# Squares of q in the up-projection: from ScalarE, in place in PSUM, to GpSimd, out of the copied q

## The chip, the cores and the metric

The kernel runs on one core of one Trainium2 chip. Five engines with queues of their own work in it: TensorE (PE, with PEld for the loading of its weights), VectorE (DVE), ScalarE (ACT), GpSimd (POOL) and SyncE (SP, which issues the DMAs). The metric is the device time of one execution in microseconds (us); less is better.

## The reference, cut to what matters

The program is one layer: a normalised input is projected, one half of the channels goes through a pooling branch, the other through latent attention, and both are gated, joined and projected back. The change lies in the latent attention, where q is made from its low-rank latent and then normalised for each head:

```
q = einsum('bsr,rd->bsd', rmsnorm(q_lat, g_q_lat), w_uq).reshape(B, S, N_HEADS, QK_HEAD)
kv = einsum('bsr,rd->bsd', rmsnorm(kv_lat, g_kv_lat), w_ukv).reshape(B, S, N_HEADS, QK_NOPE + V_HEAD)
...
q = rmsnorm(q, g_qnorm)      # over the 96 elements of a head
k = rmsnorm(k, g_knorm)
```

S is 1024 tokens, N_HEADS 8, QK_HEAD 96. So each token has 768 elements of q, and the norm needs, for each token and head, the sum of 96 squares.

## The kernel before, in words

Tokens lie on the 128 partitions in the up-projection: eight token tiles t = 0 to 7 of 128 tokens. For each tile, `up_tr(t)` turns the latent rows by three matmuls with the identity into the PSUM tile `pt` (one buffer in all), ScalarE copies it to `lth` (the part that the matmul's number format holds), and VectorE subtracts to get the rest, `ltl`. `up_tok(t)` then multiplies with the split weights: two PSUM tiles `pq` of four heads each (six matmuls each, 128 x 384), and two PSUM tiles `pk` (three matmuls each, 128 x 512), `pk0` for k and `pk1` for v. Three products stand for one: `lth` by the high weights, `lth` by the low ones, `ltl` by the high ones, so the third matmul of each group is the first that needs `ltl`.

What becomes of them, for each tile (lines of the program before):

- L550, ScalarE: `pq`, times the latent's scale `rq`, is copied to `QT[:, t]` in SBUF (twice, four heads each).
- L551, ScalarE: the square of `pq` times `rq` is written back over `pq` in PSUM (twice).
- L552, VectorE: the squares are summed over 96 elements into `ssq` (twice, 384 elements each).
- L559, VectorE: `KT[:, t]` from `pk0`; L561, ScalarE: the square of `pk0` in place; L562, VectorE: its sum into `ssq`.
- L563, ScalarE, and L564, VectorE: the two halves of `VT[:, t]` from `pk1`.

Then `up_norm` turns all of `ssq` into the factors `rqk` (L117 to L125, three Newton steps, then L573 and L574). Beside the token loop stands `gains_of_qk` (called at t = 1): small VectorE operations on a few columns, and on GpSimd eight products of 128 x 128 that make the rotation tables `TA`, `TB`, `krr`, `KB` (L512, L513). It uses 192 columns of `QT[:, 7]` as scratch before tile 7 is written. A second small chain on VectorE at the same place finishes the latents' norm (`rq`, `rlat`: L123 to L125) and the factor `rkv` (L487).

PSUM has seven banks here for `pq`, `pk` and the projections `fps` of the features, in a ring.

After the up-projection comes a stage that I call the feature stage: `fm_tile(i)` for i = 2 to 10 runs 48 matmuls of 128 x 512 for each of nine output tiles (L169), with weights that ScalarE (L146, `whi`) and VectorE (L147, `wlo`) split first; GpSimd folds the raw weights for the bias (`fm_fold`, L151 and L153). Interleaved with them is the pooling: `u` (L526, VectorE, from PSUM), running sums `s` on GpSimd (L608, L613), edges and difference on VectorE (L616, L617, L620), `dh` on ScalarE (L623), `dl` on VectorE (L624), the map `pps` on PE (L639) and its use `yp` (L640, VectorE). And on VectorE stands `up_tail(t)` for each token tile: `QT` and `KT` times `rqk` (L643, L644, L646) and the rotation (`ra`, `rbt`, L650 to L653). After it the attention runs.

The order of each engine's queue in the up-projection and the feature stage is not the order of the source: a scheduler sets it when the program is built, by its own estimates of what is ready when; from then on each engine takes its queue strictly in order. (The stage ahead and the attention stand under a schedule written by hand.)

Of the kernel before, what the change touches and what calls it, by code (L numbers as in the profile page):

```python
# [12 lines left out]
AF = mybir.ActivationFunctionType  # L13
ALU = mybir.AluOpType
AX = mybir.AxisListType
# [5 lines left out]
NK = 8  # L21
# [36 lines left out]
def body(ctx, tc, small, cond, xT, ada_sc, ada_sh, ada_gt, w_lat, w_fm, pool_w, w_uq, w_ukv, gains, pos, w_out, out):  # L58
    nc = tc.nc
    V, A, G, T, SY = nc.vector, nc.scalar, nc.gpsimd, nc.tensor, nc.sync  # L60
# [71 lines left out]
    def bk(name):  # L132
        return bank.tile([P, 512], F32, tag="b", name=name)
# [343 lines left out]
    QT = qp.tile([P, NK, H, HD], F32, tag="QT", name="QT")  # L477
    KT = qp.tile([P, NK, H, HD], F32, tag="KT", name="KT")
# [5 lines left out]
    ssq = upl.tile([P, 2, NK, H], F32, tag="ssq", name="ssq")  # L484
# [54 lines left out]
    def up_tok(t, lth, ltl):  # L539
        rq = rlat[:, 0, t:t + 1]  # L540
        rk = rlat[:, 1, t:t + 1]
        for n in range(2):
            pq = bk(f"pq{t}{n}")
            i = 0
            for j in range(2):
                for l, r in ((lth, wuqh), (lth, wuql), (ltl, wuqh)):
                    T.matmul(pq[:, :384], l[:, j, :], r[:, j, n * 384:(n + 1) * 384], start=(i == 0), stop=(i == 5))  # L547
                    i += 1
            pqv = pq[:, :384].rearrange("p (h d) -> p h d", h=4)
            A.activation(QT[:, t, n * 4:n * 4 + 4, :], pqv, AF.Copy, scale=rq)  # L550
            A.activation(pqv, pqv, AF.Square, scale=rq)  # L551
            V.tensor_reduce(ssq[:, 0, t, n * 4:n * 4 + 4], pqv, AX.X, ALU.add)  # L552
        pkv = []
        for n in range(2):
            pk = bk(f"pk{t}{n}")
            for i, (l, r) in enumerate(((lth, wkvh), (lth, wkvl), (ltl, wkvh))):
                T.matmul(pk, l[:, 2, :], r[:, n * 512:(n + 1) * 512], start=(i == 0), stop=(i == 2))  # L557
            pkv.append(pk.rearrange("p (h d) -> p h d", h=H))
        V.scalar_tensor_tensor(KT[:, t, :, 0:64], pkv[0], rk, ggk.unsqueeze(1).broadcast_to([P, H, 64]),  # L559
                               ALU.mult, ALU.mult)  # L560
        A.activation(pkv[0], pkv[0], AF.Square, scale=rk)  # L561
        V.tensor_reduce(ssq[:, 1, t, :], pkv[0], AX.X, ALU.add)  # L562
        A.activation(VT[:, t, :, 64:128], pkv[1], AF.Copy, scale=rkv[:, t:t + 1])  # L563
        V.scalar_tensor_tensor(VT[:, t, :, 0:64], pkv[1], rkv[:, t:t + 1], VT[:, t, :, 64:128],  # L564
                               ALU.mult, ALU.subtract)
        jk = upl.tile([P, 32], F32, tag="jk", name=f"jk{t}", bufs=2)
        A.activation(jk, lat[:, t, 384:416], AF.Square, accum_out=kr2[:, t:t + 1])
# [11 lines left out]
    for t in range(NK):  # L579
        if t == 1:  # L580
            gains_of_qk()
        if t == 2:
            fm_w[2] = fm_weights(2)
        nxt = up_tr(t + 1) if t + 1 < NK else None
        up_tok(t, *lt)
        lt = nxt
# [592 lines left out]
```

## Time and profile before

| | us |
|---|---|
| median of three runs | 494.69 (492.67 to 495.92) |
| the profiled execution, its own time | 494.58 |
| its span in the trace | 492.8 |
| what lies around the span | 1.8 |

| stretch of the trace (us from the start) | what runs |
|---|---|
| 84 to 117 | up-projection: tile 0 begins at 84.88 on PE, the last matmuls of tile 7 at 116.92 |
| 117 to 226 | feature stage, nine output tiles on PE |
| 226 to 493 | attention and output projection |

In the up-projection PE takes a token tile in 3.8 us. The page gives busy times of engines over the whole span; a stage is read from the rows of its own stretch of time. A row of the timeline has the start, the duration, the engine, the line, the operation, its output and inputs, and in brackets the idle time ahead of it with what ended it. Durations of neighbours on an engine overlap a little, so the distance from start to start is the better measure of what one costs.

### The profile page before, as it was taken

How to read it: one execution, taken by the hardware profiler on the slowest of the kernel's cores; microseconds unless marked ns; L12 is line 12 of the kernel's file. 1: busy time of each engine (PE TensorE's matmuls, PEld its weight loads, DVE VectorE, ACT ScalarE, POOL GpSimd, SP SyncE). 2: the span in 40 equal slices, each digit the busy share in tenths (PEclk: the TensorE clock that was granted, in tenths of full speed). 3: DMA queues.
4: the chain of work that ended last, by engine and by line, in shares of the span. 5: the costliest groups of instructions: out<-in, count | busy, mean ns of one | idle time of the engine just before them, and what ended most of it. 6: DMA issues, size and time to landing. Idle time of an engine off the chain costs nothing.

```text
span 492.8 us, 8658 instructions
## 1 busy us (share of the span) xinstructions
PE 466.9 (95%) x3468; PEld 357.2 (72%) x3468; DVE 353.4 (72%) x565; ACT 249.1 (51%) x322; POOL 222.9 (45%) x174
## 2 busy tenths in 40 slices
PE   5999998999999999999998999989999979999997
PEld 3999876898888888876565556556555658888886
DVE  4888858899999946475677887888867896813221
ACT  3756128895201111034788888788888961001000
POOL 1950031200161967736796797877959760000000
PEclk9999999899999999999999999999999999999999
DMA  8883541000102020127489879789993735743333
GB/s 294 331 323 145 171 147 53 35 2 5 50 1 92 0 91 1 43 59 156 111 136 192 171 147 182 141 168 167 208 214 57 172 140 228 273 170 129 128 129 128
DMA packets 117050, 66.40 MB, mean 135 GB/s; under 512 B 105873, under 2 KB 107793, under 8 KB 117010
## 3 DMA queue, kind: packets, MB, share of 16 engines
q1 hardware_dynamic: 117010, 65.85, 50.6%
q8 instruction: 27, 0.44, 0.4%
q14 instruction: 13, 0.11, 0.1%
HBM read 35.43 MB, written 4.19 MB: 80 GB/s over the span
## 4 chain that ended last, share of the span: by engine, by line
PE 52%; DVE 25%; ACT 7%; POOL 7%; issue 4%; DMA 4%; SPq 0%; DVEq 0%; ACTq 0%; POOLq 0%
PE ops L965 15%; PE fps L169 8%; PE st L798 6%; PE pq L547 3%; DVE bp L806 3%; POOL fraw L151 3%; ACT p L817 2%; PE rs L729 2%; DMA wlr<-in_w_lat 2%; PE pk L557 2%; PE st L802 2%; PE lps L233 2%; POOL s L613 2%; DVE ph L829 2%; ACT st L817 2%
## 5 line engine op out<-in xcount | busy, mean ns | idle before, releaser
L829 POOL TENSOR_TENSOR ph<-p,ph 128x1024 f16<-128x1024 f32 x49 | 106.2, 2176 | 12.1 <-ACT ph L822 11.7
L169 PE MATMUL fps<-xh,whi 128*128 128x512 f32 x192 | 62.0, 404 | 0.6 <-ACT whi L146 0.6
L169 PE MATMUL fps<-xh,wlo 128*128 128x512 f32 x192 | 59.3, 390 | 0.1
L169 PE MATMUL fps<-xl,whi 128*128 128x512 f32 x192 | 59.2, 390 | 0.0
L798 PE MATMUL st<-q,k 97*128 97x512 f16 x192 | 49.3, 379 | 7.3 <-ACT p L817 7.2
L822 ACT ACTIVATE ph<-p 128x1024 f16<-128x1024 f32 x49 | 51.6, 1052 | 0.5
L151 POOL TENSOR_TENSOR fraw<-fraw,shift 128x1024 f32<-128x1024 f32 x7 | 22.7, 3239 | 61.7 <-DVE wlo L147 54.8
L802 PE MATMUL st<-k,q 97*128 97x512 f16 x192 | 47.7, 379 | 1.8 <-DVE src L732 1.1
L806 DVE TENSOR_REDUCE bp<-st 128x1 f32<-128x1024 f32 x32 | 39.0, 1218 | 5.6 <-PE st L802 3.9
L169 PEld LDWEIGHTS fps<-xh,whi 128*128 128x128 f32 x192 | 35.5, 188 | 9.1 <-ACT whi L146 1.0
L169 PEld LDWEIGHTS fps<-xh,wlo 128*128 128x128 f32 x192 | 36.0, 188 | 8.0 <-DVE wlo L147 0.5
L169 PEld LDWEIGHTS fps<-xl,whi 128*128 128x128 f32 x192 | 36.1, 188 | 7.7
L817 ACT ACTIVATE p<-st,bp,esc 128x1024 f32<-128x1024 f32 x25 | 30.1, 1203 | 12.4 <-DVE bp L807 10.2
L926 ACT ACTIVATE owhi<-oraw 128x1024 fp32r<-128x1024 f32 (+1 forms) x10 | 8.8, 884 | 54.1 <-DMA oraw<-in_w_out 54.1
L798 PEld LDWEIGHTS <-k 97*128 97x128 f16 x192 | 16.6, 98 | 21.9 <-issue 8.6
L817 ACT ACTIVATE p<-st,ebias,esc 128x1024 f32<-128x1024 f32 x24 | 28.8, 1201 | 6.3 <-POOL ph L829 3.5
L623 ACT ACTIVATE dh<-s 128x1024 fp32r<-128x1024 f32 x4 | 4.3, 1064 | 52.0 <-DVE s L620 52.0
L802 PEld LDWEIGHTS <-q 97*128 97x128 f16 x192 | 16.7, 97 | 19.0 <-issue 3.9
L848 PE MATMUL av<-VT,pt 128*128 128x65 f16 x256 | 27.8, 193 | 1.3 <-DMA pt<-ph 1.3
L848 PEld LDWEIGHTS <-pt 128*128 128x128 f16 x256 | 23.7, 98 | 6.8 <-DMA pt<-ph 2.0
L850 PE MATMUL av<-VT,pt 128*128 128x65 f16 x256 | 27.7, 194 | 0.0
L849 PE MATMUL av<-VT,pt 128*128 128x64 f16 x256 | 27.6, 191 | 0.0
(299 smaller groups left out, 1227.7 us busy)
## 6 DMA issues: line engine op xcount, KB each, us to landing
fraw<-in_w_fm SPq DMA_DIRECT2D x12, 512.0 KB, 3.7
asc<-in_ada_sc SPq DMA_DIRECT2D x8, 512.0 KB, 6.2
xr<-in_xT SPq DMA_DIRECT2D x8, 512.0 KB, 5.2
ash<-in_ada_sh SPq DMA_DIRECT2D x8, 512.0 KB, 6.7
oraw<-in_w_out SPq DMA_DIRECT2D x8, 512.0 KB, 4.8
xres<-in_xT SPq DMA_DIRECT2D x8, 512.0 KB, 5.0
agt<-in_ada_gt SPq DMA_DIRECT2D x8, 512.0 KB, 5.8
out_dram<-xres SPq DMA_DIRECT2D x7, 512.0 KB, 3.0
```

What stands on the lines that cost most here:

```text
L151: G.tensor_tensor(pb, pb, shift.unsqueeze(2).broadcast_to([P, NK, P]), ALU.mult)
L169: T.matmul(ps[n], w[:, k, :], x_[k][:, n * 512:(n + 1) * 512], start=(k == order[0] and j == 0), stop=(k == order[-1] and j == 2))
L798: T.matmul(stt[i][:, n], l[:HW, kt * P:(kt + 1) * P], r[:HW, 0:512], start=(a == 0), stop=(a == 2))
L802: T.matmul(stt[i][:, n], l[:HW, qt * P:(qt + 1) * P], r[:HW, n * 512:(n + 1) * 512], start=(a == 0), stop=(a == 2))
L806: V.tensor_reduce(bps[i], stt[i], AX.XY, ALU.max)
L817: A.activation(pfs[i], st, AF.Exp, bias=bps.pop(i) if hf else ebias, scale=esc)
L822: A.activation(pas[i][:, 0], pfs[i], AF.Copy)
L829: (V if in_psum(i) else G).tensor_tensor(pas[i][:, 1], pfs[i], pas[i][:, 0], ALU.subtract)
L848: T.matmul(o_, hi, VT[:, kt, h, 64:129], start=kt == 0 and qt == 0, stop=False, skip_group_check=True)
L849: T.matmul(o_[:, 0:64], hi, VT[:, kt, h, 0:64], start=False, stop=False, skip_group_check=True)
L850: T.matmul(o_, lo, VT[:, kt, h, 64:129], start=False, stop=kt == NK - 1, skip_group_check=True)
L965: T.matmul(ps[d][n], w_[:, k, :], y_[k][:, n * 512:(n + 1) * 512], start=(k == 0 and j == 0), stop=(k == NK - 1 and j == 2))
```

## The change

For token tiles 0 to 6 the square in place (L551) and the two sums from PSUM (L552) go. In their place GpSimd multiplies the copied `QT[:, t]` by itself, all 768 elements in one instruction, and writes the squares to `KT[:, 7]`, which is free until tile 7 is made; VectorE then sums the 768 squares from there in one instruction. Tile 7 keeps the old way. One scratch serves seven tiles, so the square of a tile waits for the sum of the tile before it. The scale `rq` is in the copy already.

```
             A.activation(QT[:, t, n * 4:n * 4 + 4, :], pqv, AF.Copy, scale=rq)
-            A.activation(pqv, pqv, AF.Square, scale=rq)
-            V.tensor_reduce(ssq[:, 0, t, n * 4:n * 4 + 4], pqv, AX.X, ALU.add)
+            if t == NK - 1:
+                A.activation(pqv, pqv, AF.Square, scale=rq)
+                V.tensor_reduce(ssq[:, 0, t, n * 4:n * 4 + 4], pqv, AX.X, ALU.add)
+        if t < NK - 1:
+
+            G.tensor_tensor(KT[:, NK - 1], QT[:, t], QT[:, t], ALU.mult)
+            V.tensor_reduce(ssq[:, 0, t], KT[:, NK - 1], AX.X, ALU.add)
```

The scheduler answers with another order, and lines behind the edit stand five higher (L552 in `up_tok` becomes L557 for the new sum, L562 becomes L567, L640 becomes L645, and so on). Three places show it.

GpSimd's queue in the up-projection; `krr`, `KB`, `TA`, `TB` are the rotation tables. Before:

```order
L512 TENSOR_TENSOR krr<-krr,gn 128x8x16
L513 TENSOR_TENSOR KB<-KB,gn 128x8x16
L512 TENSOR_TENSOR TA<-krr,gn 128x8x16
L513 TENSOR_TENSOR TB<-KB,gn 128x8x16
L512 TENSOR_TENSOR TA<-krr,gn 128x8x16
L513 TENSOR_TENSOR TB<-KB,gn 128x8x16
L512 TENSOR_TENSOR krr<-krr,gn 128x8x16
L513 TENSOR_TENSOR KB<-KB,gn 128x8x16
```

And changed, where `KT<-QT` is the square:

```order
L512 TENSOR_TENSOR krr<-krr,gn 128x8x16
L513 TENSOR_TENSOR KB<-KB,gn 128x8x16
L556 TENSOR_TENSOR KT<-QT 128x768 x2
L512 TENSOR_TENSOR TA<-krr,gn 128x8x16
L513 TENSOR_TENSOR TB<-KB,gn 128x8x16
L512 TENSOR_TENSOR TA<-krr,gn 128x8x16
L513 TENSOR_TENSOR TB<-KB,gn 128x8x16
L512 TENSOR_TENSOR krr<-krr,gn 128x8x16
L513 TENSOR_TENSOR KB<-KB,gn 128x8x16
L556 TENSOR_TENSOR KT<-QT 128x768 x5
```

The squares of tiles 0 and 1 stand ahead of the six later table products, the other five behind them.

VectorE's queue at the start of the up-projection, up to `ltl` of tile 2, with what each instruction waits for (an engine's name stands for its semaphore). `pk_860` and `pk_858` are `pk0` of tile 0. Before:

```order
L562 TENSOR_REDUCE ssq<-pk_860 128x8 [waits Activation_49]
L125 SCALAR_TENSOR_TENSOR rlat<-rq_778,rlat 128x2x4 [waits DVE_49]
L501 TENSOR_SCALAR esc<-p_121 128x1
L502 TENSOR_SCALAR nesc<-p_121 128x1
L487 TENSOR_SCALAR rkv<-rlat,vsc 128x8 [waits DVE_49]
L503 RECIPROCAL ksc<-p_121 128x1
L507 TENSOR_SCALAR gn<-gn,p_121 128x32
L504 TENSOR_SCALAR ksc<-ksc 128x1 [waits DVE_49]
L536 TENSOR_TENSOR ltl_905<-pt_900,lth_904 128x384 [waits PE_49]
```

And changed:

```order
L501 TENSOR_SCALAR esc<-p_121 128x1 [waits DVE_49]
L557 TENSOR_REDUCE ssq<-KT 128x8 [waits Pool_49]
L123 TENSOR_TENSOR rq_778<-rlat 128x8 [waits DVE_49]
L567 TENSOR_REDUCE ssq<-pk_858 128x8 [waits Activation_49]
L124 SCALAR_TENSOR_TENSOR rq_778<-rq_778 128x8 [waits DVE_49]
L502 TENSOR_SCALAR nesc<-p_121 128x1
L503 RECIPROCAL ksc<-p_121 128x1
L125 SCALAR_TENSOR_TENSOR rlat<-rq_778,rlat 128x2x4 [waits DVE_49]
L507 TENSOR_SCALAR gn<-gn,p_121 128x32
L487 TENSOR_SCALAR rkv<-rlat,vsc 128x8 [waits DVE_49]
L504 TENSOR_SCALAR ksc<-ksc 128x1
L536 TENSOR_TENSOR ltl_903<-pt_898,lth_902 128x384 [waits PE_49]
```

The sum of tile 0's squares, which waits for GpSimd, now stands ahead of the last Newton steps, of the gains and of `ltl` of tile 2.

VectorE's queue in the feature stage, where the pooling's second group of channels is taken up. `u_1392` and `u_1378` are its `u`, `yp_801` the first group's result, `wlo_1429` and `wlo_1415` the weights of `fm_tile(5)`, `s_1` the second of its running sums. Before:

```order
L651 TENSOR_TENSOR rbt_1421<-QT,TB 128x256
L526 TENSOR_TENSOR u_1392<-fps_0_1326,rb 128x512
L526 TENSOR_TENSOR u_1392<-fps_1_1327,rb 128x512
L640 SCALAR_TENSOR_TENSOR yp_801<-pps_1382,small,yp_801 128x512
L640 SCALAR_TENSOR_TENSOR yp_801<-pps_1387,small,yp_801 128x512
L652 TENSOR_TENSOR QT<-ra_1420,rbt_1421 128x8x16
L653 TENSOR_TENSOR QT<-ra_1420,rbt_1421 128x8x16
L147 TENSOR_TENSOR wlo_1429<-fraw_1426,whi_1428 128x1024
L616 TENSOR_TENSOR s_1_1399<-s_1_1399,small 128x2
```

And changed:

```order
L656 TENSOR_TENSOR rbt_1407<-QT,TB 128x256
L648 TENSOR_TENSOR QT<-QT,rqk 128x768
L526 TENSOR_TENSOR u_1378<-fps_0_1312,rb 128x512
L645 SCALAR_TENSOR_TENSOR yp_801<-pps_1368,small,yp_801 128x512
L645 SCALAR_TENSOR_TENSOR yp_801<-pps_1373,small,yp_801 128x512
L526 TENSOR_TENSOR u_1378<-fps_1_1313,rb 128x512
L657 TENSOR_TENSOR QT<-ra_1406,rbt_1407 128x8x16
L658 TENSOR_TENSOR QT<-ra_1406,rbt_1407 128x8x16
L147 TENSOR_TENSOR wlo_1415<-fraw_1412,whi_1414 128x1024
L637 CAST pwh_1536<-pwr_1534 128x128
L649 TENSOR_TENSOR KT<-KT,rqk 128x8x64
L621 TENSOR_TENSOR s_1_1385<-s_1_1385,small 128x2
```

A `QT` product moved ahead of `u`, the second half of `u` moved behind the two `yp`, and `pwh` and a `KT` product moved ahead of the wait for `s_1`. Some 40 rows later, ahead of the third group's `u`, the instructions `rbt`, `QT`, `QT` (L651 to L653) of one token tile likewise moved from behind it to ahead of it.

## The prediction
> **What bounds the kernel now.** I read the page first, for the whole; then the busy times by stage; then PE's rows where it waits, and the chain of waits backward from there; last the timeline of the queues that the change touches.
>
> The page's span and busy times, and PE and VectorE in three stretches (busy us and instructions of each engine, granted clock, DMA):
>
> ```profile
> span 492.8 us, 8658 instructions
> PE 466.9 (95%) x3468; PEld 357.2 (72%) x3468; DVE 353.4 (72%) x565; ACT 249.1 (51%) x322; POOL 222.9 (45%) x174
> 89.00:117.00 28.00, 27.96 (x153) 25.19 (x152) 26.18 (x64) 25.88 (x52) 3.43 (x8) 1.00 0.00 1
> 117.00:211.00 94.00, 94.00 (x419) 77.46 (x418) 74.23 (x136) 16.59 (x19) 49.80 (x34) 1.00 0.11 37
> 211.00:227.00 16.00, 15.37 (x67) 11.67 (x67) 10.76 (x19) 5.26 (x7) 5.97 (x10) 1.00 0.45 98
> ```
>
> In the up-projection (first stretch) PE, ScalarE and VectorE are all over 92% busy, GpSimd 12%. In the feature stage PE is full for 94 us, and only behind it does it pause. That pause decides this case. PE's rows there, and the chain of waits that leads to them:
>
> ```profile
> 211.07 0.40 PE L639 MATMUL pps<-dh,pwl 128*128 128x512 f32 x1
> 212.04 0.74 PE L169 MATMUL fps<-xh,whi 128*128 128x512 f32 x2 [0.58 <-ACT whi L146]
> 213.31 0.50 PE L169 MATMUL fps<-xh,wlo 128*128 128x512 f32 x1
> ...
> 159.99 1.14 DVE wlo L147
> 161.20 10.00 POOL fraw L151
> 180.86 0.16 DVE s L616
> 187.35 1.91 POOL fraw L151
> 200.60 2.37 POOL s L613
> 202.99 1.23 DVE s L616
> 212.03 1.24 DVE wlo L147
> ```
>
> PE would go on at 211.3, waits for `whi`, and gets `wlo` at 213.31. Back from there the chain runs without a gap through `wlo`, GpSimd's sums, the fold at 161.20, and VectorE, whose timeline shows no idle time from 116 to 174. So although PE looks like the bound, the end of the feature stage is set by VectorE and GpSimd, with PE about 1.1 us late (211.3 plus the two matmul pairs that need no `wlo`, 0.9, would be 212.2). Whatever makes VectorE late at 117 comes out at 213; whatever makes it early gains at most that 1.1 us.
>
> **Removed.** ScalarE loses 14 squares, VectorE has seven long sums for 14 short ones:
>
> ```profile
> L551 ACT ACTIVATE pq<-pq,rlat x16: 547/560/582, 89.9 to 116.9; 128x384 f32<-128x384 f32 x16
> 105.45 0.69 DVE L562 TENSOR_REDUCE ssq<-pk 128x8 f32<-128x512 f32 x1 [0.40 <-ACT pk L561]
> 106.06 1.01 DVE L552 TENSOR_REDUCE ssq<-pq 128x4 f32<-128x384 f32 x2
> 106.99 0.74 DVE L559 SCALAR_TENSOR_TENSOR KT<-pk,rlat,ggk 128x512 f32<-128x512 f32 x1
> 107.65 0.74 DVE L564 SCALAR_TENSOR_TENSOR VT<-pk,rkv,VT 128x512 f16<-128x512 f32 x1
> 108.31 0.55 DVE L536 TENSOR_TENSOR ltl<-pt,lth 128x384 fp32r<-128x384 f32 x1
> ```
>
> 14 x 0.56 = 7.8 us leave ScalarE, but it is no longer than PE there, and no wait of PE in this stretch names it; I cost that at nothing (cover: PE's own 3.8 us per tile). On VectorE, start to start, a 384 sum takes 0.465, a 512 sum 0.61: 1.13 ns per element, so 768 take about 0.90, against 0.93 for the pair: equal. Per tile VectorE's work is 0.61 + 0.93 + 0.66 + 0.66 + 0.48 = 3.34 us before and 3.31 after, so half a us of a tile's 3.8 can absorb waits. The trace has no long sum from SBUF; were the new one free of the PSUM sums' fixed part, it would still cost 0.87, so I bound the gain at 0.5 us for all seven. The Trainium skill ("VectorE: DVE Perf Modes", the cycle table of the section on SBUF-source ops) gives 58 cycles plus the elements from SBUF and 120 plus the elements from PSUM: by that the pair costs 1.05 us, the long sum 0.86, and the stage would gain 1.3 us of VectorE time where I count 0.2. Here the 384 sum's 0.465 us is below its 0.525, so I keep the row.
>
> **Added: the square and its place in two queues.** The nearest row (the first) is an operation of the same size, the next the page's group of a larger one; then the rows of the startup and of the lock:
>
> ```profile
> 228.31 1.54 POOL L710 TENSOR_TENSOR src1h<-QT,src1h 128x768 f16<-128x768 f32 x1
> L829 POOL TENSOR_TENSOR ph<-p,ph 128x1024 f16<-128x1024 f32 x49 | 106.2, 2176 | 12.1 <-ACT ph L822 11.7
> 90.70 0.46 POOL L513 TENSOR_TENSOR KB<-KB,gn 128x128 f32<-128x128 f32 x1
> 93.79 0.55 DVE L536 TENSOR_TENSOR ltl<-pt,lth 128x384 fp32r<-128x384 f32 x1
> 94.39 0.55 PE L531 MATMUL pt<-ident,lat 128*128 128x128 f32 x3
> 122.47 2.06 POOL L608 TENSOR_TENSOR s<-u 128x1038 f32<-128x1038 f32 x1 [4.95 <-DVE rqk L112]
> 122.80 1.89 DVE L124 SCALAR_TENSOR_TENSOR rh<-rh 128x128 f32<-128x128 f32 x1
> ```
>
> The last two show the lock: a Newton step that takes 0.29 elsewhere took 1.89 because GpSimd was in an addition. VectorE operations with two SBUF inputs and GpSimd's exclude each other. (Those that read PSUM do not: the rows of `ltl` and the sums at 93.8 to 96 keep their length beside GpSimd's table products.)
>
> Startup, term A. GpSimd is free at 91.16, squares tile 0 until 92.7; the sum, ahead of everything else in VectorE's new order, ends at 93.6 (`QT`'s first copy starts at 89.4, both are done by 90.7). Then the square of tile 1 runs to 95.2 and holds the Newton step behind the k sum; the seven small instructions behind it take 0.6 as before, so `ltl` of tile 2 starts at 95.9 instead of 93.79. PE's `pt` of tile 3 waits for it (one buffer): 96.5 for 94.39. One matmul moved ahead of `pt` and a gap already there give back 0.4, so PE enters tile 2 about 1.7 late. Queued behind `ltl` are the `VT` halves, which hold PSUM banks; PE asks for those a tile later, so they add nothing.
>
> Steady tiles. With tile 4 of the trace:
>
> ```profile
> 102.49 0.42 PE L547 MATMUL pq<-wuqh,lth 128*128 128x384 f32 x1
> 106.06 0.49 PE L531 MATMUL pt<-ident,lat 128*128 128x128 f32 x3
> L550 ACT ACTIVATE QT<-pq,rlat x16: 574/583/592, 89.4 to 116.4; 128x384 f32<-128x384 f32 x16
> 119.96 0.33 DVE KB L520
> ```
>
> From the tile's start: the last `pq` ends at 2.25, its copy at 2.85, the square at 4.45 (1.54 and a handoff), then VectorE's sum 5.35, `VT` 6.0, k sum 6.6, `ltl` of two tiles on 7.1. PE asks for that `ltl`'s buffer at 3.81 + 3.57 = 7.4. So it holds, with 0.3 to spare; the wait of VectorE for GpSimd (0.5 to 0.7 a tile) is covered by its spare half us, nearly. I take one slip of 0.3. At the end `krr` (L519), now ahead of tile 6's sum, has two SBUF inputs and can stand behind the square of tile 6, which the next sum waits for anyway. VectorE reaches `KB` (119.96 before) 1.65 late if nothing more slips and 2.6 late if `krr` is held a full us. Term A: 2.2. Its bounds: 0.5 (no lock on the Newton step, waits all hidden), 3.
>
> **Moved in the feature stage.** Two places where VectorE and GpSimd overlapped:
>
> ```profile
> 144.07 1.28 DVE L526 TENSOR_TENSOR u<-fps,rb 128x512 f32<-128x512 f32 x2
> 145.49 1.92 POOL L608 TENSOR_TENSOR s<-u 128x1038 f32<-128x1038 f32 x1 [4.51 <-DVE u L526]
> 147.49 2.04 POOL L613 TENSOR_TENSOR s<-s 128x1036 f32<-128x1036 f32 x1
> 145.35 1.32 DVE yp L640 x2
> 142.54 0.60 DVE KT L644
> 152.23 0.87 DVE QT L643
> 150.54 0.15 DVE L616 TENSOR_TENSOR s<-s,small 128x2 f32<-128x2 f32 x1
> 169.35 1.27 DVE L526 TENSOR_TENSOR u<-fps,rb 128x512 f32<-128x512 f32 x2
> ```
>
> Term B. Before, GpSimd's two additions begin with `u` and run partly beside the two `yp`, which read PSUM. In the new order `u` is complete only after `QT` 0.87, `u` 0.60, `yp` 1.32, `u` 0.60: 144.07 + 3.4 = 147.46. From there all takes turns: GpSimd 1.92 + 1.93, VectorE `QT`, `QT` 0.4, `wlo` 1.13, `pwh` 0.14, `KT` 0.6: 6.1 us, to 153.6, for 150.54 before. Work that now lies ahead is 0.87 + 0.14 + 0.60 = 1.6, so the loss is 1.5. It does not depend on who goes first. Bounds: 0 (if GpSimd shares), 2.
>
> Term C. The fold at 161.20 stood behind VectorE's unbroken run of two-input products until `u` at 169.35 let it in. Three of them (0.34 + 0.20 + 0.20) now stand ahead of that `u`: 0.7. Bounds: -0.9 (that of the `QT` that left the run), 1.2. The Trainium skill ("SBUF — State Buffer", "Who interferes with whom") says that whoever starts first has the shared ports for one whole instruction. By that the fold waits for one product only, VectorE's `u` comes later instead, and C would be about 1.1; the row's 10.00 us, eight of them waiting, speaks for a longer hold.
>
> **Sum.** 2.2 + 1.5 + 0.7 = 4.4 us, all on the chain that ends at 213.31, where no slack is left; behind it PE is full to 226 and the attention follows in a fixed order, so it reaches the end. 494.58 + 4.4 = 499.0, against the profiled execution's own time, which is 0.1 below the median shown. That is 0.9%; I call a change measurable from 1% (4.9 us), so the likeliest verdict is no change, on the slow side.
>
> **Rivals.**
> - Slower by over 1%: the square is longer than I take. Place: the loop copy, square, sum, `ltl`. Slack 0.3, so it decides from about 1.9 us. At 2.2 (what the page's group `ph` takes for 128 x 1024) five tiles slip 0.3 each: 1.5 more, 500.5; at 3, 504. For it: the same addition took 2.06 at 122.47 and 1.92 at 145.49, so GpSimd is stretched by company. Against it: 1.54 for the same size. Chance 0.33 with the upper end of my own terms.
> - Hidden: the sums fill VectorE's idle half us, the Newton step slips between two squares, A falls to 0.5: 494.58 + 0.5 + 2.2 = 497.3; with B shared too, 495.5. For it: PE's stretch is full now. Chance 0.17.
> - Faster: ScalarE's 7.8 us free the banks sooner, VectorE ends early by its 0.5, and PE's pause at 211 shrinks: 494.0, at best 494.58 - 1.1 = 493.5, and more only if the order of the attention's work also fell better. Against it: PE is full from 89 to 211 already. Chance 0.05, of it 0.02 for over 1%.
>
> **Numbers.** My forecast holds 0.45, the rivals 0.33, 0.17 and 0.05. Time 499.0; range 495.4 (hidden, shared) to 502.5 (a square of about 2.6 us). That leaves out the faster case and a part of the hidden one below, and the long squares above, about 0.1 each. Faster by over 1% 0.02, within 0.45 + 0.17 + 0.03 = 0.65, slower 0.33.
>
> **What would show it.** A: `ltl` of tile 2 near 96 and PE's `pt` waiting for it; squares of 1.5 us; VectorE idle 0.5 ahead of each new sum. B: `wlo` of `fm_tile(5)` and its neighbours stretched, the s row at 153.6 + A. C: the third `u` 0.7 later again. PE's waits in the feature stage grow to near 4 us. Wrong if PE's `pt` never waits, if the VectorE chain ends the stage early, or if the attention's own length changes.

## The result, and the profile after

| | before | after |
|---|---|---|
| median, us (runs) | 494.57 (4 runs) | 499.55 (4 runs) |
| lowest to highest | 492.67 to 495.92 | 499.10 to 501.21 |
| the profiled execution, its span | 492.8 | 499.4 |

The ratio is 1.0118, with a 95% interval of 1.0091 to 1.0145: the change costs 1.2%. (In a second series, below, it was 1.0087, 1.0054 to 1.0120.) The page of the profile after, its span and the busy times:

```profile
span 499.4 us, 8644 instructions
PE 469.4 (94%) x3468; PEld 358.3 (72%) x3468; DVE 357.8 (72%) x558; ACT 243.9 (49%) x308; POOL 234.3 (47%) x181
```

The windows of the profile after, the three stretches of the prediction (busy us and instructions of PE, PEld, VectorE, ScalarE, GpSimd; granted clock, DMA share, GB/s):

```profile
89.00:117.00 28.00, 26.05 (x141) 23.15 (x141) 25.43 (x53) 18.84 (x34) 13.48 (x15) 1.00 0.00 1
117.00:211.00 94.00, 92.89 (x413) 76.15 (x412) 76.66 (x136) 16.58 (x20) 50.73 (x35) 1.00 0.11 37
211.00:227.00 16.00, 14.65 (x63) 11.22 (x62) 12.16 (x21) 5.26 (x5) 5.18 (x5) 1.00 0.16 46
```

ScalarE is 7.0 us lighter in the up-projection (25.88 to 18.84), GpSimd 10 us heavier (3.43 to 13.48), as meant. But PE, which had no gap there, now has 1.95 us of them. Where they come from is in the timeline of GpSimd, VectorE and PE, at the start and the end of the up-projection:

```profile
91.67 1.48 POOL L556 TENSOR_TENSOR KT<-QT 128x768 f32<-128x768 f32 x1
91.81 1.36 DVE L125 SCALAR_TENSOR_TENSOR rlat<-rq,rlat 128x8 f32<-128x8 f32 x1
93.18 0.95 DVE L557 TENSOR_REDUCE ssq<-KT 128x8 f32<-128x768 f32 x1
94.72 1.04 DVE L124 SCALAR_TENSOR_TENSOR rq<-rq 128x8 f32<-128x8 f32 x1
96.23 0.55 DVE L536 TENSOR_TENSOR ltl<-pt,lth 128x384 fp32r<-128x384 f32 x1
96.83 0.55 PE L531 MATMUL pt<-ident,lat 128*128 128x128 f32 x3 [1.53 <-DVE ltl L536]
...
101.49 0.95 DVE L557 TENSOR_REDUCE ssq<-KT 128x8 f32<-128x768 f32 x1 [0.81 <-POOL KT L556]
108.60 0.55 PE L531 MATMUL pt<-ident,lat 128*128 128x128 f32 x3 [0.25 <-DVE ltl L536]
116.03 1.46 DVE L519 TENSOR_TENSOR krr<-lat,krr 128x256 f32<-128x256 f32 x1
119.72 0.50 PE L562 MATMUL pk<-wkvh,lth 128*128 128x512 f32 x1 [0.50 <-DVE VT L569]
123.04 0.40 DVE L520 TENSOR_TENSOR KB<-lat,KB 128x256 f32<-128x256 f32 x1
```

The same places in the timeline of before (the second matmul of tile 2, then `krr` and `KB`), and the second matmul of tile 2 after:

```profile
95.13 0.34 PE L547 MATMUL pq<-wuql,lth 128*128 128x384 f32 x1
119.54 0.42 DVE L519 TENSOR_TENSOR krr<-lat,krr 128x256 f32<-128x256 f32 x1
119.87 0.42 DVE L520 TENSOR_TENSOR KB<-lat,KB 128x256 f32<-128x256 f32 x1
```

```profile
97.13 0.42 PE L547 MATMUL pq<-wuql,lth 128*128 128x384 f32 x1
```

Two Newton steps that take 0.16 undisturbed are held by squares (1.36 and 1.04), the sum stands ahead of `ltl`, and PE waits 1.53 for `ltl` of tile 2. Later VectorE waits 0.8 ahead of a sum, `krr` takes 1.46 for 0.42 beside the square of tile 6, and PE waits twice more (0.25 at 108.60, 0.50 at 119.72). The feature stage after, same view:

```profile
148.25 0.68 DVE L526 TENSOR_TENSOR u<-fps,rb 128x512 f32<-128x512 f32 x1
150.16 0.68 DVE L526 TENSOR_TENSOR u<-fps,rb 128x512 f32<-128x512 f32 x1
150.98 3.91 POOL L613 TENSOR_TENSOR s<-u 128x1038 f32<-128x1038 f32 x1 [6.69 <-DVE u L526]
154.97 1.92 POOL L618 TENSOR_TENSOR s<-s 128x1036 f32<-128x1036 f32 x1
156.92 0.16 DVE L621 TENSOR_TENSOR s<-s,small 128x2 f32<-128x2 f32 x1 [3.81 <-POOL s L618]
...
166.86 9.45 POOL L151 TENSOR_TENSOR fraw<-fraw,shift 128x1024 f32<-128x1024 f32 x1 [8.16 <-DVE wlo L147]
174.13 0.42 DVE L656 TENSOR_TENSOR rbt<-QT,TB 128x256 f32<-128x256 f32 x1
174.59 1.87 DVE L657 TENSOR_TENSOR QT<-ra,rbt 128x128 f32<-128x128 f32 x1
176.59 1.28 DVE L526 TENSOR_TENSOR u<-fps,rb 128x512 f32<-128x512 f32 x2
186.10 0.17 DVE L621 TENSOR_TENSOR s<-s,small 128x4 f32<-128x4 f32 x1 [1.87 <-POOL s L618]
...
217.21 0.73 PE L169 MATMUL fps<-xh,whi 128*128 128x512 f32 x2 [0.84 <-ACT whi L146]
```

The addition at 150.98 took 3.91 for 1.92, until VectorE had no product left, and VectorE then waited 3.81 for GpSimd. The fold at 166.86, which takes 1.9 alone, stood 7.6 us.

To compare traces that begin their work a little apart, I count from the first `pq` matmul of tile 0 (84.88 before, 85.22 after) to four marks: `KB` (L520), the first `s` row of the second and third pooling group (L616 before, L621 after), and the first `rs` matmul, with which the attention begins.

One thing has to be taken out first. In some executions PE's clock is halved right at the start of the up-projection. The same window of two traces, of the profile after and of a kernel below (`e2`) whose up-projection is that of before; the third number from the end is the granted clock:

```profile
86.00:88.00 2.00, 2.00 (x6) 1.60 (x6) 2.00 (x15) 1.69 (x8) 0.00 (x0) 0.50 0.77 258
```

```profile
86.00:88.00 2.00, 2.00 (x12) 1.57 (x11) 2.00 (x17) 1.79 (x5) 0.00 (x0) 1.00 0.61 229
```

The profiles before and after both have this dip, so they compare. Where the up-projection is otherwise unchanged, `KB` comes 34.99 after the first `pq` with the dip (before) and 33.56 without (`e2`): it costs 1.43, which I take off the marks of before for traces without a dip. (`e7`, whose up-projection is also that of before, has 33.52.) The dip does not fall on the same matmuls each time, and the changed kernel's `KB` is at 37.82 in one trace and 37.53 in the other, so marks of two traces compare to about 0.3. The Trainium skill ("TensorE: Matmul & The Clock Gate", "What's actually happening") says that the clock is either full or half, decided in free-running windows of about 3.4 us. The trace agrees: the mean clock from 85 to 89 is 0.57 after, which is 3.4 us at half.

A run's mean clock moves its time too. A straight line through the 194 fast runs of this study whose clock is on record (one run of `e2`, 502.18 us, was slow and is left out), with one offset for each kernel and one slope, gives 0.43 us per 0.001 of clock (runs lie between 0.986 and 1.000). Some kernels had their runs at lower clocks than others, so the table has each kernel's offset from the kernel before at equal clock, with its 95% interval, beside the plain ratio. The runs of the experiments come from three chips; the same line drawn for each chip alone moves no offset by more than 0.4.

| kernel | dip | `KB` | 2nd `s` | 3rd `s` | first `rs` | `rs` late by | time over before at equal clock | ratio, 95% interval |
|---|---|---|---|---|---|---|---|---|
| before | yes | 34.99 | 65.66 | 95.98 | 141.55 | | | |
| before, less 1.43 | no | 33.56 | 64.23 | 94.55 | 140.12 | | | |
| after | yes | 37.82 | 71.70 | 100.88 | 146.43 | 4.88 | 4.2 ± 0.4 (with e10) | 1.0118, 1.0091 to 1.0145 |
| e10 the same again | yes | 37.53 | 71.40 | 100.58 | 146.04 | 4.49 | | 1.0087, 1.0054 to 1.0120 |
| e1 order back | yes | 37.70 | 68.49 | 98.83 | 144.42 | 2.87 | 2.9 ± 0.6 | 1.0104, 1.0073 to 1.0134 |
| e2 order alone | no | 33.56 | 67.28 | 96.46 | 141.99 | 1.87 | 1.8 ± 0.4 | 1.0048, 1.0029 to 1.0066 |
| e3 sums behind | no | 34.61 | 65.43 | 95.75 | 142.31 | 2.19 | 1.7 ± 0.4 | 1.0043, 1.0025 to 1.0062 |
| e4 idle squares | no | 34.58 | 65.40 | 95.73 | 141.34 | 1.22 | 1.3 ± 0.4 | 1.0034, 1.0011 to 1.0056 |
| e5 tile 0 back | no | 33.91 | 64.71 | 95.03 | 141.59 | 1.47 | 1.3 ± 0.4 | 1.0039, 1.0016 to 1.0062 |
| e6 idle scalings | yes | 34.93 | 65.76 | 96.08 | 141.66 | 0.11 | 0.0 ± 0.4 | 0.9993, 0.9977 to 1.0009 |
| e7 `whi` first | no | 33.52 | 64.19 | 94.52 | 138.86 | -1.26 | -1.7 ± 0.4 | 0.9972, 0.9954 to 0.9990 |
| e8 both | no | 33.92 | 64.74 | 95.07 | 140.42 | 0.30 | 0.4 ± 0.4 | 1.0006, 0.9984 to 1.0028 |
| e9 free bank | yes | 36.63 | 67.46 | 97.78 | 142.11 | 0.56 | -1.3 ± 0.4 | 0.9981, 0.9956 to 1.0006 |

From these rows: the changed kernel is 2.83 late at `KB`, and 4.90 at the third `s`; then nothing is added (4.88 at `rs`). Of the 6.04 at the second `s`, 1.61 is work that now lies ahead of it, so 4.43 count there: 1.60 more than at `KB`, and 0.47 more come by the third. The profiled execution was the longest of its four and lost another 1.4 in the attention (267.75 from `rs` to the end, 266.37 before): its clock dipped a second time there, to a mean of 0.84 from 410 to 420. In e10, the same kernel, the two marks that matter come out alike: 2.54 late at `KB`, 1.59 more at the second `s`, 0.47 more at the third.

### The profile page after: what moved, and what is told of

It is laid out like the page before. It is cut to its first block, busy times and chain, and to the rows that moved or that the text cites. A ratio compares the mean times of both kernels' runs of the same rounds, so it can differ in the third digit from the quotient of the medians.

```text
span 499.4 us, 8644 instructions
## 1 busy us (share of the span) xinstructions
PE 469.4 (94%) x3468; PEld 358.3 (72%) x3468; DVE 357.8 (72%) x558; ACT 243.9 (49%) x308; POOL 234.3 (47%) x181
## 4 chain that ended last, share of the span: by engine, by line
PE 53%; DVE 25%; ACT 7%; POOL 6%; issue 4%; DMA 4%; SPq 0%; DVEq 0%; ACTq 0%; POOLq 0%
PE fps L169 15%; PE ops L970 15%; PE st L803 5%; PE st L807 3%; DVE bp L811 3%; DMA wlr<-in_w_lat 2%; ACT p L822 2%; PE rs L734 2%; PE lps L233 2%; POOL fraw L151 2%; DVE yq L914 1%; POOL ph L834 1%; DVE ph L834 1%; ACT st L822 1%; DMA pt<-ph 1%
## 5 line engine op out<-in xcount | busy, mean ns | idle before, releaser
L853 PE MATMUL av<-VT,ph 128*128 128x65 f16 x256 | 27.6, 193 | 0.0
```

Source lines behind the costliest of these rows:

```text
L853: T.matmul(o_, hi, VT[:, kt, h, 64:129], start=kt == 0 and qt == 0, stop=False, skip_group_check=True)
```

## The experiments

My theory was three separate losses: A in the up-projection, where VectorE's queue passes waits for GpSimd's squares on to PE; and B and C in the feature stage, where the same instructions stand in another order. The rivals were that the order alone costs the time (PE being full in the up-projection and absorbing its delay), that the up-projection alone costs it, and that GpSimd's company costs it wherever the sums stand.

The first two kernels hold VectorE's queue to a list. The numbers are those of its instructions counted from `krr` (L519); the added edges order the queue and make nothing wait:

```
+DVE_ORDER = (223, 195, 196, 186, 191, 224, 225, 231, 201, 202, 352, 203, 353, 382, 383, 207, 384, 387, 388,
...
+def keep_order(tc, nc, first):
+    n0 = int(first.name[2:])
+    dve = {int(i.name[2:]) - n0: i for i in nc.cur_bb.bb.instructions
+           if i.engine == first.engine and i.name[2:].isdigit()}
+    for p, q in zip(DVE_ORDER, DVE_ORDER[1:]):
+        tc.add_manual_dep(dve[q], dve[p].name,
+                          mybir.DependencyInfo(mybir.DependencyClass.NoSync, mybir.DependencyReason.DATA),
+                          reason="order")
```

### e1: the up-projection's part alone

The changed kernel with that list, the order of before from the second group's `u` to the third group's sums.

> The changed kernel, with VectorE's queue in the feature stage (from the second group's u to the third group's sums) held in the order of the kernel before: the up-projection's part of the change alone. My theory (three separate losses, A in the up-projection, B and C from the other order in the feature stage): KB is 2.8 us late against the kernel before, the s row of the second group is as late and no later, and the time is 494.6 + 2.8 = 497.4 (496.8 to 498.0). Rival 1, the feature stage's order alone costs time, since PE's full queue absorbs the up-projection: 494.6. Rival 2, the up-projection alone costs it and the order is harmless: 499.5.

Measured: 498.59 (6 runs) against 493.67 on the same chip, a ratio of 1.0104. Taken plainly, that is 4.9 and the second rival. But these six runs had a mean granted clock of 0.9925, those of before 0.998; at equal clock it is 2.9 ± 0.6, as the theory has it. The trace does not need that correction, since it is compared with a trace of the same dip: `KB` 2.71 late, the second `s` 2.83, the third 2.85, `rs` 2.87. What is late at `KB` comes out unchanged at the attention, and nothing is added. The first rival falls. This run does not tell which engine carries the delay: PE itself ends the up-projection 2.91 late (its last `pk` matmul, 34.95 after the first `pq` for 32.04).

### e2: the order alone

The kernel before with the changed kernel's list; not one instruction of the up-projection differs.

> The kernel before, without any change in the up-projection, with VectorE's queue in the feature stage held in the order of the changed kernel: terms B and C alone. My theory: KB where it was, the s row of the second group 1.6 us late beside the 1.6 of work that now lies ahead of it, the third group's s row about 2.1 late, time 494.6 + 2.1 = 496.7 (496.0 to 497.2). The order alone (rival 1): 499.5. Harmless order (rival 2): 494.6.

Measured: 1.8 ± 0.4 at equal clock, the plain ratio 1.0048. Its timeline, GpSimd and VectorE:

```profile
146.12 3.90 POOL L608 TENSOR_TENSOR s<-u 128x1038 f32<-128x1038 f32 x1 [6.69 <-DVE u L526]
152.05 0.16 DVE L616 TENSOR_TENSOR s<-s,small 128x2 f32<-128x2 f32 x1 [3.81 <-POOL s L613]
161.99 9.45 POOL L151 TENSOR_TENSOR fraw<-fraw,shift 128x1024 f32<-128x1024 f32 x1 [8.16 <-DVE wlo L147]
169.72 1.87 DVE L652 TENSOR_TENSOR QT<-ra,rbt 128x128 f32<-128x128 f32 x1
181.23 0.16 DVE L616 TENSOR_TENSOR s<-s,small 128x4 f32<-128x4 f32 x1 [1.87 <-POOL s L613]
```

These are the durations of the changed kernel (3.91, 3.81, 9.45, 1.87), without its up-projection. The second `s` is 3.05 late, less 1.61 of moved work 1.44: B. The third is 1.91 late: C is 0.47. PE ends this up-projection on time, so here it is the chain through VectorE and GpSimd that makes the attention late. The theory is confirmed and the second rival falls; 2.87 and 1.87 add up to 4.74, the change itself is 4.88 and 4.49 late in its two traces.

### e3: the sums behind `ltl`

The order of e1, and seven edges that put the sum of tile t behind `ltl` of tile t + 2, and `krr` behind the last k sum. The last edge undoes the move of `krr`.

```
+SUMS_BEHIND = ((-281, -329), (-234, -263), (-193, -216), (-152, -175), (-111, -134), (-70, -93), (-6, 0))
...
-    for p, q in zip(DVE_ORDER, DVE_ORDER[1:]):
+    for p, q in [*SUMS_BEHIND, *zip(DVE_ORDER, DVE_ORDER[1:])]:
```

> The changed kernel with the feature stage's order of before and with each of VectorE's new sums put behind the ltl of the tile after next, krr back behind the last k sum: GpSimd squares as much as in the change, but VectorE no longer stands waiting for it ahead of an ltl. My theory (VectorE's in-order queue passes the wait on): only the Newton step held by the first square is left, 1.1 us less PE's 0.4 of slack, so KB 0.7 late and 494.6 + 0.7 = 495.3 (494.6 to 496.0). Rival, GpSimd's squares slow the others wherever the sums stand: as with the first of these kernels, 497.4.

Measured: 1.7 ± 0.4, between the two. The trace divides it: `KB` is 1.05 late instead of 2.71, and stays so to the third `s` (1.20); from there to `rs` another 1.0 is lost. So the sums' place and `krr` account for 1.66 of A. A part of that comes by way of GpSimd's queue: the square of tile 1 waits for the sum of tile 0, so it now stands behind the six table products (93.96), where it holds no Newton step. What the other 1.0 ahead of the attention is, e5 and e9 show.

### e4: the squares' company alone

The kernel before, with squares that nobody reads:

```
+        if t < NK - 1:
+            G.tensor_tensor(KT[:, NK - 1], QT[:, t], QT[:, t], ALU.mult)
```

> The kernel before with seven squares of q on GpSimd that nobody reads, added to its own sums; every engine's queue is otherwise as before: the squares' company alone. My theory: a Newton step held by the first square, 1.1 us less PE's 0.4, no wait of VectorE for GpSimd after that: 495.3 (494.6 to 495.8). Rival, the squares' company is most of the up-projection's loss (VectorE's instructions or PE's matmuls get longer beside them): 2 us or more, 496.6 to 497.4.

Measured: 1.3 ± 0.4; `KB` 1.02 late, `rs` 1.22. The 1.02 is made at one place, in the timeline:

```profile
89.62 1.47 POOL L554 TENSOR_TENSOR KT<-QT 128x768 f32<-128x768 f32 x1
89.89 1.22 DVE L125 SCALAR_TENSOR_TENSOR rlat<-rq,rlat 128x8 f32<-128x8 f32 x1
91.73 0.48 PE L559 MATMUL pk<-wkvh,lth 128*128 128x512 f32 x1 [0.57 <-DVE rq L123]
```

One Newton step takes 1.22 for 0.16, and PE waits for what follows it already at the `pk` of tile 1. The 0.4 of slack that I had subtracted belongs to the changed kernel's PE queue, where a matmul moved ahead of `pt`; this kernel has the queue of before and is 1.01 late from that `pk` on. The other six squares hold nothing on the path (`KB` is no later than this one step). Squares cost by what they meet, not by being there.

### e5: tile 0 by ScalarE

e3, with the place of e4's loss taken away:

```
-            if t == NK - 1:
+            if t in (0, NK - 1):
...
-        if t < NK - 1:
+        if 0 < t < NK - 1:
```

> As the kernel with the sums behind ltl, and tile 0 squared by ScalarE and summed in two short sums as before the change, so that GpSimd squares tiles 1 to 6 only and nothing runs beside the startup's Newton steps. My theory (the 1.1 to 1.2 us that the two kernels with unhurried sums still lost are one Newton step held by the first square, 1.22 or 1.36 us for 0.16): ltl of tile 2 and KB where they were, and the time of the kernel before, within 0.4 at equal granted clock. Rival (each square costs a little): six sevenths of it are left, 1.0 over the kernel before.

Measured: 1.3 ± 0.4, which looks like the rival. The trace says otherwise: `ltl` of tile 2 is where it was (7.43 after the first `pq`, 7.44 in e2), `KB` is 0.35 late, the third `s` 0.48; what that 0.35 is, I did not find out (PE ends the up-projection on time, 30.63 after the first `pq` for 30.61 in e2). Then comes the same 1.0 as in e3, here in the timeline of VectorE and PE:

```profile
222.89 0.68 DVE L526 TENSOR_TENSOR gT<-fps,rb 128x512 f32<-128x512 f32 x1
223.62 0.50 PE L169 MATMUL fps<-xh,whi 128*128 128x512 f32 x1 [0.77 <-DVE gT L526]
```

By the programs' allocations the last feature tile (`fps11`) is written to PSUM banks 4 and 5. In the kernel before, tile 10, whose halves are evicted (`gT`) just ahead, lies in banks 3 and 1; in e3 and e5 it lies in 1 and 5. The ring of banks goes on from the up-projection, and there, by my reading, the sums' new place lets go of the banks in another order; e9 tests it. So PE waits for an eviction 100 us behind the edit.

### e6: a lock, but between which operations

e4 with one input in place of two:

```
-            G.tensor_tensor(KT[:, NK - 1], QT[:, t], QT[:, t], ALU.mult)
+            G.tensor_scalar(KT[:, NK - 1], QT[:, t], 2.0, None, ALU.mult)
```

> The kernel before with seven idle operations on GpSimd as in the kernel of the idle squares, but each reads one tensor (q times 2.0) in place of q times q; nobody reads them. If the lock is between VectorE's two-input products and any SBUF operation of GpSimd (rival): the Newton step beside the first is held as before, 1 us, and the time is 1.1 over the kernel before. If it takes an operation of two inputs on GpSimd's side too (my theory, from rows that show only such): the Newton step stays at 0.16 and the time is that of the kernel before within 0.4.

Measured: 0.0 ± 0.4, `rs` 0.11 late.

```profile
90.27 2.14 POOL L554 TENSOR_SCALAR KT<-QT 128x768 f32<-128x768 f32 x1
90.93 0.18 DVE L125 SCALAR_TENSOR_TENSOR rlat<-rq,rlat 128x8 f32<-128x8 f32 x1
91.72 0.14 DVE L124 SCALAR_TENSOR_TENSOR rq<-rq 128x8 f32<-128x8 f32 x1
```

The operation is longer (2.14 for 1.47), covers the same Newton steps, and holds none. The Trainium skill ("SBUF — State Buffer", "Who interferes with whom") says that a VectorE instruction with two SBUF inputs contends with a GpSimd instruction that reads SBUF; in these rows the GpSimd operation with one input does not hold it, and the rows decide. They are two small steps of one run.

### e7 and e8: the pause at 211

The kernel before, with the order of before and one edge on ScalarE (651 is the activation of `gT`, 656 is `whi` of the tenth weight tile); e8 has the same edge on e5.

```
+    act = {int(i.name[2:]) - n0: i for i in nc.cur_bb.bb.instructions
+           if i.engine == mybir.EngineType.Activation and i.name[2:].isdigit()}
+    tc.add_manual_dep(act[651], act[656].name,
+                      mybir.DependencyInfo(mybir.DependencyClass.NoSync, mybir.DependencyReason.DATA),
+                      reason="order")
```

> The kernel before with two instructions of ScalarE exchanged at the end of the feature stage: whi of the tenth weight tile ahead of the bias and activation of gT, so that PE's pause at 211 no longer waits for ScalarE's queue. My theory: whi starts near 209.8 for 210.95, wlo ends 1.1 earlier, the pause is gone, and the time is 1.1 below the kernel before (492.6 where that is 493.7). Rival: gT is wanted, or whi's buffer is free, no earlier, and the time is unchanged.

> The repaired change (tile 0 by ScalarE, the sums behind ltl, the feature stage's order of before) and the exchange on ScalarE together. My theory: the repaired change costs nothing and brings nothing, since PE is the bound in the up-projection, so the time is that of the exchange alone, 1.1 below the kernel before. Rival: GpSimd's squares bring something once nothing waits for them, and it is below the exchange alone by over 0.5.

Measured for e7: a ratio of 0.9972 (0.9954 to 0.9990), 1.7 ± 0.4 below the kernel before at equal clock: more than I expected. ScalarE in the timeline of before:

```profile
206.22 1.06 ACT L623 ACTIVATE dh<-s 128x1024 fp32r<-128x1024 f32 x1 [17.94 <-DVE s L620]
209.90 1.15 ACT L675 ACTIVATE gT<-gT,bias_fm 128x1024 f32<-128x1024 f32 x1 [2.62 <-DVE gT L526]
210.95 1.04 ACT L146 ACTIVATE whi<-fraw 128x1024 fp32r<-128x1024 f32 x1
```

And e7, ScalarE, VectorE and PE:

```profile
204.65 1.06 ACT L623 ACTIVATE dh<-s 128x1024 fp32r<-128x1024 f32 x1 [17.95 <-DVE s L620]
205.61 1.04 ACT L146 ACTIVATE whi<-fraw 128x1024 fp32r<-128x1024 f32 x1
208.15 1.22 DVE L147 TENSOR_TENSOR wlo<-fraw,whi 128x1024 fp32r<-128x1024 f32 x1
209.53 0.40 PE L639 MATMUL pps<-dh,pwl 128*128 128x512 f32 x1
209.77 0.63 PE L169 MATMUL fps<-xh,whi 128*128 128x512 f32 x2
```

`whi` starts not 1.1 but 3.8 earlier against `dh` (0.96 behind its start, at 205.61, for 4.73): it could have run all that time but stood behind `gT`, which itself waited for VectorE. PE waits neither for `whi` nor for `wlo` any more. e8 is 0.4 ± 0.4 above the kernel before, where I expected 1.1 below: its stretch from the third `s` to `rs` is 1.0 longer than that of e7 (45.35, 44.34), which is the bank of e5, and no gain of the squares appears.

### e9: the same with another bank

e8 without the edge for tile 1's sum, by which tile 10 comes to lie in banks 1 and 2.

```
-SUMS_BEHIND = ((-234, -263), (-193, -216), (-152, -175), (-111, -134), (-70, -93), (-6, 0))
+SUMS_BEHIND = ((-193, -216), (-152, -175), (-111, -134), (-70, -93), (-6, 0))
```

> As the kernel with both edits, with one more difference that follows from leaving tile 1's sum where the change put it: the evictions of the up-projection end in another order, so that the last feature tile but one has its second half in PSUM bank 2 and not in bank 5, which the last feature tile (fps11) writes next. My theory (of the 1.5 us that the repaired change still lost ahead of the attention, 1.0 is PE at 222 waiting for the eviction of that bank, which has nothing to do with the squares): that wait is gone, the first rs starts 1.0 earlier against the first pq, and the time is 1.2 below the kernel before (1.6 gained by the exchange, 0.4 lost). Rival (the squares cost it in another way): 0.2 to 0.5 above the kernel before, as the kernel with both edits at equal clock.

Measured: 1.3 ± 0.4 below the kernel before at equal clock, as expected, though its plain ratio (0.9981) cannot be told from 1: that agreement rests on the correction for the clock. PE at the place of the wait, from its timeline:

```profile
222.80 0.28 PE L159 MATMUL psb<-ones,fraw 128*128 128x1 f32 x2
222.94 0.71 PE L169 MATMUL fps<-xh,whi 128*128 128x512 f32 x2
```

No wait; from the third `s` to `rs` it takes 44.33 where e8 takes 45.35. That shows the bank's part. But `rs` came 0.56 later than before in this trace and not earlier, because the clock dip had put a square elsewhere:

```profile
92.48 1.47 POOL L556 TENSOR_TENSOR KT<-QT 128x768 f32<-128x768 f32 x1 [2.43 <-ACT QT L550]
92.48 1.50 DVE L507 TENSOR_SCALAR gn<-gn,p 128x32 f32<-128x32 f32 x1
94.56 0.55 PE L531 MATMUL pt<-ident,lat 128*128 128x128 f32 x3 [1.08 <-DVE ltl L536]
```

PE ran at half clock, tile 1's copy came late, and its square, which met nothing in e5, met a small operation of 0.22 and held it 1.28 longer. The repair thus depends on a few tenths of a us.

### e10: the change again

The changed kernel, unaltered.

> The changed kernel itself, unaltered, in as many runs as the others, since it had four: 4.8 above the kernel before (4.4 to 5.3) at equal granted clock by my theory, the sum of 2.9 for the up-projection's part alone and 1.9 for the order alone; if the two parts disturbed each other, more than 0.7 away from that.

Measured: 498.51 (7 runs) against 493.79, a ratio of 1.0087; with the first four runs 4.2 ± 0.4 at equal clock, `rs` 4.49 late. The middle lies just below the 4.4 to 5.3 that I expected; it agrees with the sum of the parts, 4.7, within the errors; a part of a us in which A and the order disturb or help each other is not excluded.

## Why the prediction was right, point by point

The time, 499.0, is 0.5 below the median measured, and the cause is the one it named. That it came so near is in part luck: A was 0.6 too small, C 0.2 too large, and the plain difference (4.98) and that at equal clock (4.2 ± 0.4) lie on both sides of the 4.4 forecast. Whether the change costs less than 1%, which I held likeliest, stays open: 1.18% in the first series, 0.87% in the second.

- **What bounds the kernel.** Right: in e2 PE ends the up-projection on time, and VectorE's order alone makes the attention 1.87 late. e1 would look the same if PE carried A, since PE is late there by as much. And the end of the feature stage was set by the order of ScalarE's queue as well: of the pause at 211 the prediction blamed VectorE and GpSimd, and e7 took it away without touching either's sums.
- **Removed.** Right. ScalarE's relief bought nothing that shows. The long sum takes 0.87 from its start to the next instruction's (0.90 taken).
- **The square.** 1.47 for 1.54. The main rival, a longer square, did not occur.
- **A, 2.2 taken, 2.83 measured (2.54 in e10).** Mechanism right, size off. `ltl` of tile 2 was foreseen 2.1 late and is 2.10 late (96.23 less 85.22, against 93.79 less 84.88). PE then enters tile 2 1.66 late (97.13 less 85.22, against 95.13 less 84.88) where I had about 1.7, so the 0.4 that I gave back is there. The terms that were too small come later. The slip of 0.3 is 0.48 at tile 5 (PE's last `pk` matmul of a tile is 1.80 late at tile 4 and 2.28 at tile 5). And `krr` was held 1.04 longer than its 0.42: with a full us I had named 2.6 and then took 2.2. Its delay went on to `VT`, and PE waited 0.50 for that bank at 119.72, a wait that I had considered for the startup alone.
- **B, 1.5 taken, 1.60 and 1.44 measured** (the change, e2). The two engines took turns as described.
- **C, 0.7 taken, 0.47 measured** in both. The three products ahead of `u` stood there, but the fold did not wait for `u` as I had it. It got in behind the first of the three, in a gap of about 0.1 us ahead of `QT` at 174.59: one product (0.34) and the gap make the 0.47.
- **A sign that failed.** PE's idle time in the feature stage was to grow to near 4 us. It grows from 0.6 (117.3 to 226.4 before) to 2.0 (119.7 to 231.6 after), since PE brings A's delay along from the up-projection.
- **Hidden.** The rival that A falls to 0.5 is refuted for this order by e1, and shown for another by e5 (0.35 at `KB`). Its time with B shared, by its own terms 494.58 + 0.5 + 0.7 = 495.8, was written as 495.5.
- **Faster.** It did not occur, and where nothing waits for the squares any more (e5, e8) no gain of ScalarE's relief shows either.

## What to carry to other kernels

An engine that has time to spare is no free place for work if the results come back through the queue of an engine without any: here seven squares of 1.5 us, for which GpSimd had the time, made the up-projection 2.8 us longer. Of that, 1.66 went with the place of the sums and of `krr` in VectorE's queue, and most of the rest was one Newton step held by the first square. Where a scheduler sets the order, look at the order of all that follows: 1.9 of some 4.7 us came from instructions that the edit didn't touch, and a repair can lose 1 us to a PSUM bank 100 us on. And a pause that seems to belong to the slowest chain may lie in a queue that holds ready work behind something that waits: exchanging two instructions of ScalarE (e7) brought 1.7 us.

## What the runs showed of the hardware

- A GpSimd operation that waits for the lock does not get it between VectorE's products, though nineteen of them began while it stood: 7.6 us of the 9.45, in all three traces with that order (after, e10, e2). It got in where a start came 0.46 after the last one and 0.33 is usual (174.13, 174.59); that the gap let it in is my reading.
- Of two GpSimd operations of the same size, that with one input is slower, 2.14 for 1.47, and held nothing (e6). A TENSOR_SCALAR of VectorE on SBUF was held as its two-input products are (1.50 for 0.22, e9).
- PE's clock was halved for 3.4 us in six of the twelve profiles, at the same place, the start of the up-projection; four (after, e1, e3, e7) have such a dip in the attention. None of the 17 runs of the changed kernel and e1 had a mean clock of 0.999 or more, 36 of 82 of the kernel before did. Whether PE's added pauses cause that was not tried; if so, it would be part of the change's cost that the comparison at equal clock leaves out.
